# The order of seven products: A12 B21 moved from ahead of U + S3 T3 to behind it, and A12 split into high and low parts together with A22

## The chip, the cores and the metric

The kernel runs on one core of one Trainium2 chip. The metric is device time in microseconds, from the start of the program to its end, as the median of several runs. A program has five engines that work side by side, each through its own queue and in that queue's order: TensorE (matmuls and the loads of their stationary operand), VectorE, ScalarE, GpSimd and SyncE. SyncE's queue issues the loads of the weights. They wait for each other by semaphores. Matmul results go to PSUM, which has 8 banks of 128 x 512 fp32 here; everything else lies in SBUF.

## The reference

The reference is a small decoder trunk: 2 layers, 512 tokens, width 1024, hidden width 2816. A layer is half an FFN, a mixer (gated linear attention in the first layer, stick-breaking attention in the second) and half an FFN again, each on a normalised input. So there are four FFNs:

```python
def swiglu(h, w_gate, w_up, w_down):
    return (jax.nn.silu(h @ w_gate) * (h @ w_up)) @ w_down

for i in range(DEPTH):
    x = x + 0.5 * swiglu(rmsnorm(x, ffn1_norm[i]), ffn1_w_gate[i], ffn1_w_up[i], ffn1_w_down[i])
    h = rmsnorm(x, mix_norm[i])
    y = gla_mixer(h, ...) if i % 2 == 0 else sb_mixer(h, ...)
    x = x + y
    x = x + 0.5 * swiglu(rmsnorm(x, ffn2_norm[i]), ffn2_w_gate[i], ffn2_w_up[i], ffn2_w_down[i])
return rmsnorm(x, final_norm)
```

All inputs and outputs are float32.

## The kernel before, in words

**Three matmuls for one.** Activations are kept transposed, features by tokens (128 x 512 tiles). To be close to float32, every operand is split into a high and a low part in the fast matmul type (fp32r): ScalarE casts the high part (L126 for weights), VectorE subtracts it from the original to get the low part (L127). A product is then three matmuls: high x high, low x high, high x low.

**The feed.** All weight work stands in one long list of entries (`feed.q`). An entry has units (pieces of a raw weight chunk, or sums of pieces, to be split) and a body, a generator whose `yield`s divide its matmuls into steps. `Feed.start` (L139) starts the next entry: it splits the units of up to three entries ahead, as long as no more than four large units (1024 elements a partition) are in hand, makes the sums of four ahead and issues the loads of six ahead, which go to the SP queue (L91). Large split weights have four buffers for the high and four for the low parts (tags "wh", "wl"); a unit under 1024 elements goes to a single small buffer, "vh" and "vl", one of each (L116, L117). A raw chunk of 1 MB has two buffers.

**Who sets the order.** A planner orders the instructions of each engine when the program is built, by priority in program order and by its own estimate of when things are ready. For TensorE in the seven-product chunks the order is given: `feed.entries(n, True)` (L173) pins each step's TensorE instructions behind the last matmul of the step before (`issue_after`). ScalarE and VectorE are not pinned there.

**The seven-product chunks.** In an FFN, 9 of the 11 gate chunks and 9 of the 11 up chunks (256 columns each) are computed with seven products of half-size blocks instead of eight: 72 chunks in the four FFNs. `seven` (L664) cuts a chunk's weights into A11 and A12 (first 128 columns; first and second half of the input features) and A21, A22 (last 128 columns), and the tokens into two halves of 256. Each product is 4 feature tiles x 3 matmuls = 12 matmuls with 256 columns. S1 to S4 are sums of blocks of the weights (`sums_12`, `sums_34`), T1 to T4 sums of blocks of the input, made once in each FFN. Three accumulators are used, each half a bank: w, q and z. The steps, by line of the kernel before:

| product | accumulator | then |
|---|---|---|
| A11 B11 (L714) | w, new | ScalarE copies w into z (L715) |
| S1 T1 (L717) | q, new | ScalarE copies q into o1 (L718) |
| S2 T2 (L720) | w, added: U | ScalarE copies w into o0 (L721) |
| A12 B21 (L723) | z, added to the copy | the gate: SiLU on ScalarE (L701) or a multiply on VectorE (L704) |
| S3 T3 (L731) | w, added: U + S3 T3 | ScalarE copies w into u3 (L733), VectorE adds it to o1 (L734) |
| S4 B22 (L736) | q, added | VectorE adds q to o0 (L737), gates |
| A22 T4 (L743) | w, added | gate |

The first four are `body_1`, an entry with the units [A11 and A12 together, S1 and S2]; the last three are `body_2`, the next entry, with the units [S3 and S4, A22]. A22 is 512 elements a partition and goes to the small buffer. The accumulators take the 8 banks in turn (L44). Where the entry before a chunk is not of this kind, the very first matmul uses a 128 x 128 copy of its weights cast for it alone (`lead`, L129 to L133).

**What stands between the chunks.** Down projections: `down` entries (24 matmuls of 512 columns, L313), and, for one hidden group in each FFN, `seven_down` (L331), which also has seven products (L367), two entries, and an A22 of 512 elements that goes to the same small buffer and is used in its last step. It comes in two parts in each FFN; part 0 is followed at once by the next gate chunk, part 1 by a `down` entry.

Of the kernel before, what the change touches and what calls it, by code (L numbers as in the profile page):

```python
# [18 lines left out]
P = 128  # L19
T = 512  # L20
D = 1024
KD = D // P
# [6 lines left out]
NEAR, NEAR_MOVING = 16, 48  # L29
# [3 lines left out]
def decoder(ctx: ExitStack, tc: tile.TileContext, a: dict, out: bass.AP):  # L33
# [13 lines left out]
    def psum(name, tag=None):  # L47
        if tag is None:
            tag = order[turn_[0] % 8]
            turn_[0] += 1  # L50
        return pp.tile([P, T], F32, tag=tag, bufs=banks[tag], name=name)
# [130 lines left out]
    feed = Feed()  # L182
# [405 lines left out]
    class FFN:  # L588
# [75 lines left out]
        def seven(self, ch, group=None):  # L664

            H = T // 2
            s12, v = [None], {}  # L670

            def sums_12(t):
                s = s12[0] = self.tp.tile([P, KD, P], F32, tag="s", bufs=4, name="s12")
                nc.vector.tensor_tensor(out=s[:, 0:4], in0=t[:, 0:4, P:], in1=t[:, 4:8, P:], op=ALU.add)
                nc.vector.tensor_tensor(out=s[:, 4:8], in0=s[:, 0:4], in1=t[:, 0:4, 0:P], op=ALU.subtract)
                return s

            def sums_34(t):
                s = self.tp.tile([P, KD, P], F32, tag="s", bufs=4, name="s34")
                nc.vector.tensor_tensor(out=s[:, 0:4], in0=t[:, 0:4, 0:P], in1=t[:, 0:4, P:], op=ALU.subtract)  # L680
                nc.vector.tensor_tensor(out=s[:, 4:8], in0=t[:, 4:8, 0:P], in1=s12[0][:, 4:8], op=ALU.subtract)
                return s

            def prod(o, w, w0, b, first=True, lead=None):
                for j in range(4):
                    bh, bl = b(j)
                    wh, wl = w[0][:, w0 + j], w[1][:, w0 + j]
                    for n, (l_, r_) in enumerate(((wh, bh), (wl, bh), (wh, bl))):
                        if lead is not None and j + n == 0:
                            l_ = lead  # L690
                        st["pe"] = nc.tensor.matmul(  # L691
                            o, l_, r_, start=first and j + n == 0, stop=j == 3 and n == 2, skip_group_check=True
                        ).ins

            def half(k0, c):
                return lambda j: (st["h"][k0 + j][:, c * H : c * H + H], st["l"][k0 + j][:, c * H : c * H + H])

            def gate(o, c, t):

                if group is None:  # L700
                    st["silu"] = nc.scalar.activation(o[:, c : c + H], t, AF.Silu).ins  # L701
                else:
                    g = self.gates[0 if o is v["o"][0] else 1]
                    nc.vector.tensor_tensor(out=o[:, c : c + H], in0=t, in1=g[:, c : c + H], op=ALU.mult)  # L704

            def body_1(W):


                ax, s = W
                v["w"], v["q"] = psum("ps_w"), psum("ps_q")  # L710
                z = psum("ps_z")[:, 0:H]
                w, q = (v[n][:, 0:H] for n in "wq")
                o0, o1 = v["o"] = [self.tp.tile([P, T], F32, tag="t", name=n) for n in ("o0", "o1")]
                prod(w, ax, 0, half(0, 0), lead=entry.first if lead else None)  # L714
                nc.scalar.copy(z, w)  # L715
                yield
                prod(q, s, 0, lambda j: self.t_half(0, j))  # L717
                nc.scalar.copy(o1[:, H:T], q)  # L718
                yield
                prod(w, s, 4, lambda j: self.t_half(1, j), first=False)  # L720
                nc.scalar.copy(o0[:, H:T], w)  # L721
                yield
                prod(z, ax, 4, half(4, 0), first=False)  # L723
                gate(o0, 0, z)
                yield

            def body_2(W):
                s, a22 = W
                w, q = (v[n][:, 0:H] for n in "wq")
                o0, o1 = v["o"]  # L730
                prod(w, s, 0, lambda j: self.t_half(2, j), first=False)  # L731
                u3 = self.tp.tile([P, H], F32, tag="c", bufs=1, name="u3")
                nc.scalar.copy(u3, w)  # L733
                nc.vector.tensor_tensor(out=o1[:, H:T], in0=u3, in1=o1[:, H:T], op=ALU.add)  # L734
                yield
                prod(q, s, 4, half(4, 1), first=False)  # L736
                nc.vector.tensor_tensor(out=o0[:, H:T], in0=q, in1=o0[:, H:T], op=ALU.add)  # L737
                gate(o0, H, o0[:, H:T])
                if group is not None:
                    close_0(o0)  # L740
                gate(o1, H, o1[:, H:T])
                yield
                prod(w, a22, 0, lambda j: self.t_half(3, j), first=False)  # L743
                gate(o1, 0, w)
                if group is not None:
                    close_1(o0, o1)
                    del self.gates[:2]
                else:
                    self.gates += [o0, o1]
                yield  # L750

            def close_0(o0):
                if group in self.DOWN_SEVEN:
                    self.close_first(o0, group)
                else:
                    self.close(o0, group)

            def close_1(o0, o1):
                if group in self.DOWN_SEVEN:
                    self.close_second(o0, o1, group)  # L760
                else:
                    self.close(o1, group)


            lead = feed.q[-1].place != NEAR
            entry = Entry([(ch, lambda t: t[:, :, 0:P], KD, P), (ch, sums_12, KD, P)], body_1, NEAR, lead)
            feed.q.append(entry)
            feed.q.append(Entry([(ch, sums_34, KD, P), (ch, lambda t: t[:, 4:8, P:], 4, P)], body_2, NEAR))

        def t_half(self, i, j):  # L770

# [963 lines left out]
```

## Time and profile before

| | |
|---|---|
| time, median of 3 runs | 1848.96 us (1847.21 to 1850.33) |
| the profiled execution's own time | 1846.76 us |
| its span, first to last instruction | 1844.9 us |
| granted TensorE clock, mean | 0.999 |
| TensorE busy | 1829.8 us, 12188 matmuls |
| weight loads busy | 1651.2 us |
| VectorE busy | 1477.4 us |
| ScalarE busy | 1039.4 us |
| GpSimd busy | 8.7 us |

How to read it: busy time is the time in which an engine executed at least one instruction; matmuls overlap, so their starts tell the pace better than their durations. PE is TensorE's matmuls, PEld its weight loads, DVE VectorE, ACT ScalarE, POOL GpSimd, SP SyncE. A row of a group gives the line, the engine, the operation, the tiles (output <- inputs) and the count. "[0.72 <-ACT u L733]" behind an instruction says that its engine was idle for 0.72 us before it and that the ScalarE instruction of line 733, which writes u, let it go on. L126 <- raw is a cast of weights as loaded, L126 <- s one of a sum.

### The profile page before, as it was taken

To read this page: it belongs to the slowest core of one execution; us is meant where nothing else is said; L and a number is where in the kernel's file an instruction comes from. 1 tells how busy PE (TensorE), PEld (TensorE's weight loads), DVE (VectorE), ACT (ScalarE), POOL (GpSimd) and SP (SyncE) were. 2 spreads that over 40 slices of the span, in tenths; PEclk is the share of its full clock that TensorE was granted. 3 is DMA by queue.
4 is the path that set the end of the run, shared out by engine and by line. 5 is a ranking of instruction groups with operands and counts; after the bars stand their busy time and mean duration, and the time that the engine had idled before them with its cause. 6 is when DMAs were issued, how large, how long until landed. Compare 5 with 4: busy or idle time off the path is not lost.

```text
span 1844.9 us, 29917 instructions
## 1 busy us (share of the span) xinstructions
PE 1829.8 (99%) x12188; PEld 1651.2 (89%) x12188; DVE 1477.4 (80%) x2345; ACT 1039.4 (56%) x1782; POOL 8.7 (0%) x20
## 2 busy tenths in 40 slices
PE   8999999999999999999999999999999999999998
PEld 7999989889888899999889999998888788999997
DVE  8999776776787989877798997676878779897775
ACT  6556445444555556544555555455888755664454
POOL 0000000100000000000000000000000000000000
PEclk9999999999999999999999999999999999999999
DMA  5333333221223333333233233322222123333321
GB/s 162 121 119 115 103 115 113 81 69 47 69 69 114 92 110 97 126 103 104 86 109 115 92 115 115 100 85 80 69 69 61 65 92 93 114 124 103 118 80 69
DMA packets 177645, 179.16 MB, mean 97 GB/s; under 512 B 4130, under 2 KB 168020, under 8 KB 177508
## 3 DMA queue, kind: packets, MB, share of 16 engines
q1 hardware_dynamic: 176800, 176.18, 30.4%
q8 instruction: 95, 1.56, 0.4%
q0 software_dynamic: 608, 1.05, 0.2%
q14 instruction: 42, 0.34, 0.1%
q10 hardware_dynamic: 100, 0.03, 0.0%
HBM read 175.17 MB, written 2.10 MB: 96 GB/s over the span
## 4 chain that ended last, share of the span: by engine, by line
PE 89%; DVE 7%; DMA 3%; ACT 1%; issue 1%; SPq 0%; ACTq 0%; DVEq 0%
PE ps_d L66 20%; PE ps_w L691 18%; PE ps_f L66 18%; PE ps_q L691 9%; PE ps_t L66 5%; PE ps_z L691 5%; PE ps_b L66 4%; DVE wl L127 2%; DMA raw<-in_ffn_w_up_dram 2%; PE ps_w L367 1%; PE ps_S L66 1%; PE ps_z L1314 1%; PE ps_bt L66 1%; PE ps_oT L1376 1%; DMA raw<-in_ffn_w_gate_dram 1%; PE ps_T L1361 1%
## 5 line engine op out<-in xcount | busy, mean ns | idle before, releaser
L127 DVE TENSOR_TENSOR wl<-raw,wh 128x1024 fp32r<-128x1024 f32 x242 | 256.9, 1065 | 88.2 <-ACT wh L126 53.8
L126 ACT CAST wh<-raw 128x1024 fp32r<-128x1024 f32 (+1 forms) x242 | 223.2, 923 | 152.7 <-PE ps_d L66 44.4
L691 PE MATMUL ps_w<-th,wh 128*128 128x256 f32 x864 | 239.9, 278 | 2.3 <-ACT u L733 1.6
L691 PE MATMUL ps_w<-tl,wh 128*128 128x256 f32 x864 | 238.9, 276 | 0.0
L691 PE MATMUL ps_w<-th,wl 128*128 128x256 f32 x864 | 238.9, 276 | 0.0
L127 DVE TENSOR_TENSOR wl<-s,wh 128x1024 fp32r<-128x1024 f32 x160 | 195.4, 1223 | 49.3 <-PE ps_z L691 37.6
L126 ACT CAST wh<-s 128x1024 fp32r<-128x1024 f32 x160 | 168.2, 1052 | 113.2 <-PE ps_d L66 28.9
L66 PE MATMUL ps_d<-hh,wl 128*128 128x512 f32 x544 | 212.1, 390 | 0.0
L66 PE MATMUL ps_d<-hh,wh 128*128 128x512 f32 x544 | 211.9, 390 | 0.0
L66 PE MATMUL ps_d<-hl,wh 128*128 128x512 f32 x544 | 211.6, 389 | 0.0
L66 PE MATMUL ps_f<-xh,wh 128*128 128x512 f32 x432 | 172.7, 400 | 0.1
L66 PE MATMUL ps_f<-xl,wh 128*128 128x512 f32 x432 | 169.5, 392 | 0.0
L66 PE MATMUL ps_f<-xh,wl 128*128 128x512 f32 x432 | 168.9, 391 | 0.0
L691 PEld LDWEIGHTS ps_w<-th,wh 128*128 128x128 f32 x864 | 162.4, 188 | 4.1 <-ACT u L733 3.3
L691 PEld LDWEIGHTS ps_w<-tl,wh 128*128 128x128 f32 x864 | 162.2, 188 | 0.0
L691 PEld LDWEIGHTS ps_w<-th,wl 128*128 128x128 f32 x864 | 162.2, 188 | 0.0
L126 ACT CAST wh<-rawd 128x1024 fp32r<-128x1024 f32 (+1 forms) x84 | 85.1, 1014 | 121.3 <-PE ps_d L66 82.6
L322 DVE SCALAR_TENSOR_TENSOR x<-ps_d,x 128x512 f32<-128x512 f32 x152 | 102.7, 689 | 56.7 <-PE ps_d L66 56.2
L127 DVE TENSOR_TENSOR wl<-rawd,wh 128x1024 fp32r<-128x1024 f32 (+1 forms) x84 | 98.3, 1174 | 41.6 <-ACT wh L126 24.4
L66 PEld LDWEIGHTS ps_d<-hl,wh 128*128 128x128 f32 x544 | 102.1, 188 | 21.5
L66 PEld LDWEIGHTS ps_d<-hh,wh 128*128 128x128 f32 x544 | 102.1, 188 | 20.3
L66 PEld LDWEIGHTS ps_d<-hh,wl 128*128 128x128 f32 x544 | 102.1, 188 | 19.7
(348 smaller groups left out, 4880.2 us busy)
## 6 DMA issues: line engine op xcount, KB each, us to landing
raw<-in_ffn_w_gate_dram SPq DMA_DIRECT2D x43, 1024.0 KB, 5.4
raw<-in_ffn_w_up_dram SPq DMA_DIRECT2D x43, 1024.0 KB, 5.4
rawd<-in_ffn_w_down_dram SPq DMA_DIRECT2D x84, 512.0 KB, 3.6
raw<-in_gla_w_in_dram SPq DMA_DIRECT2D x12, 1024.0 KB, 5.3
raw<-in_sb_w_in_dram SPq DMA_DIRECT2D x16, 512.0 KB, 3.7
raw<-in_gla_w_out_dram SPq DMA_DIRECT2D x4, 1024.0 KB, 5.0
raw<-in_sb_w_in_dram SPq DMA_DIRECT2D x4, 1024.0 KB, 5.1
raw<-in_sb_w_out_dram SPq DMA_DIRECT2D x4, 1024.0 KB, 5.0
```

The costliest lines, as they stand in the source:

```text
L66: st["pe"] = nc.tensor.matmul(ps, l, r, start=first, stop=last).ins
L126: st["cut"] = nc.scalar.copy(h, r).ins
L127: nc.vector.tensor_tensor(out=l, in0=r, in1=h.bitcast(F32), op=ALU.subtract)
L322: nc.vector.scalar_tensor_tensor(out=xs[k], in0=ps, scalar=0.5, in1=xs[k], op0=ALU.mult, op1=ALU.add)
L367: st["pe"] = nc.tensor.matmul(ps, l_, r_, start=first and c + n == 0, stop=c == 1 and n == 2, skip_group_check=True).ins
L691: st["pe"] = nc.tensor.matmul(o, l_, r_, start=first and j + n == 0, stop=j == 3 and n == 2, skip_group_check=True).ins
L1314: nc.tensor.matmul(o_, l_, r_, start=first, stop=last, skip_group_check=True)
L1361: nc.tensor.transpose(ps[:, c0 : c0 + P], ys[yb][:, yc + j * P : yc + (j + 1) * P], ident)
L1376: nc.tensor.matmul(po[e * 64 : e * 64 + 64, j * P : T], self.v[j][:, c : c + 64], self.wt[p, e][bk][:, c0 : c0 + n], start=j == 0, stop=j ...
```

## The change

A12 B21 moves from the end of `body_1` to `body_2`, where it stands as a step of its own between U + S3 T3 and S4 B22. `body_1` has three products then and `body_2` four; z is kept between them in `v["z"]`. With it A12 changes its unit: the first entry splits A11 alone (4 x 128 = 512 elements, which goes to the small buffer) with S1 and S2; the second splits S3 and S4, and A12 with A22 as one piece of 4 x 256 = 1024 elements, a large buffer. `prod` gets a column offset `c0` so that A22 is found in the second 128 columns of that piece. The number of matmuls, casts, subtractions, sums and loads stays, and so do the total elements that are split. `seven_down` is not touched.

```diff
-            def prod(o, w, w0, b, first=True, lead=None):
+            def prod(o, w, w0, b, first=True, lead=None, c0=0):
                 for j in range(4):
                     bh, bl = b(j)
-                    wh, wl = w[0][:, w0 + j], w[1][:, w0 + j]
+                    wh, wl = (t[:, w0 + j, c0 : c0 + P] for t in w)
...
             def body_1(W):
-                ax, s = W
+                a11, s = W
                 v["w"], v["q"] = psum("ps_w"), psum("ps_q")
-                z = psum("ps_z")[:, 0:H]
+                z = v["z"] = psum("ps_z")[:, 0:H]
...
-                prod(w, ax, 0, half(0, 0), lead=entry.first if lead else None)
+                prod(w, a11, 0, half(0, 0), lead=entry.first if lead else None)
                 nc.scalar.copy(z, w)
                 yield
...
                 prod(w, s, 4, lambda j: self.t_half(1, j), first=False)
                 nc.scalar.copy(o0[:, H:T], w)
                 yield
-                prod(z, ax, 4, half(4, 0), first=False)
-                gate(o0, 0, z)
-                yield
 
             def body_2(W):
-                s, a22 = W
+                s, a2 = W
...
                 prod(w, s, 0, lambda j: self.t_half(2, j), first=False)
                 u3 = self.tp.tile([P, H], F32, tag="c", bufs=1, name="u3")
                 nc.scalar.copy(u3, w)
                 nc.vector.tensor_tensor(out=o1[:, H:T], in0=u3, in1=o1[:, H:T], op=ALU.add)
+                yield
+
+                prod(v["z"], a2, 0, half(4, 0), first=False)
+                gate(o0, 0, v["z"])
                 yield
                 prod(q, s, 4, half(4, 1), first=False)
...
-                prod(w, a22, 0, lambda j: self.t_half(3, j), first=False)
+                prod(w, a2, 0, lambda j: self.t_half(3, j), first=False, c0=P)
                 gate(o1, 0, w)
...
-            entry = Entry([(ch, lambda t: t[:, :, 0:P], KD, P), (ch, sums_12, KD, P)], body_1, NEAR, lead)
+            entry = Entry([(ch, lambda t: t[:, 0:4, 0:P], 4, P), (ch, sums_12, KD, P)], body_1, NEAR, lead)
             feed.q.append(entry)
-            feed.q.append(Entry([(ch, sums_34, KD, P), (ch, lambda t: t[:, 4:8, P:], 4, P)], body_2, NEAR))
+            feed.q.append(Entry([(ch, sums_34, KD, P), (ch, lambda t: t[:, 4:8], 4, 256)], body_2, NEAR))
```

## The prediction

> **What bounds the kernel now.** I read the page's first part, then what TensorE waits for, then the line of the seven-product chunks (L691) and the ScalarE copies that read its accumulators. First the page and the waits of TensorE (engine, line, releaser: us in total, times, longest):
>
> ```profile
> span 1844.9 us, 29917 instructions
> PE 1829.8 (99%) x12188; PEld 1651.2 (89%) x12188; DVE 1477.4 (80%) x2345; ACT 1039.4 (56%) x1782; POOL 8.7 (0%) x20
> PEclk9999999999999999999999999999999999999999
> ```
> ```profile
> PE ps_x L1571 <- DMA x<-in_x_dram: 4.3, 2, 3.8
> PE ps_w L691 <- ACT u L733: 1.6, 3, 0.7
> PE ps_f L1596 <- ACT wh L1541: 0.6, 1, 0.6
> PE ps_w L691 <- ACT ps_z L715: 0.4, 2, 0.2
> ```
>
> TensorE is busy for 99% of the span and hardly waits once the inputs have landed. So a change pays only by fewer or denser matmuls, and every microsecond for which TensorE is made to wait is added whole. This change keeps all matmuls. What it moves are the copies which stand between two uses of one accumulator. The same line with the waits of weight loads added (times in ns min/median/max; then idle us, times):
>
> ```profile
> L691 PE MATMUL ps_w<-th,wh x864: 276/276/388, 71.6 to 1806.6; 128*128 128x256 f32 x173
>   ACT u L733: 4.9, 10
>   ACT ps_z L715: 1.2, 4
> ```
>
> Now one chunk's second half of step 1, where U (the third product) ends and A12 B21 (into z) begins, with the ScalarE copy that reads U out of w:
>
> ```profile
> 122.30 0.28 PE L691 MATMUL ps_w<-tl,wh 128*128 128x256 f32 x1
> 122.41 0.28 PE L691 MATMUL ps_z<-nh,wh 128*128 128x256 f32 x1
> ...
> 122.61 0.37 ACT L721 COPY o<-ps_w 128x256 f32<-128x256 f32 x1 [0.99 <-PE ps_w L691]
> ...
> 123.66 0.28 PE L691 MATMUL ps_z<-nl,wh 128*128 128x256 f32 x1
> 123.77 0.28 PE L691 MATMUL ps_w<-th,wh 128*128 128x256 f32 x1
> ```
>
> Matmuls start 0.113 us apart (122.30, 122.41), and a product of 12 takes 1.36 (122.41 to 123.77). The copy of U runs from 122.61 to 122.98, while TensorE fills z; w is next wanted at 123.77, 0.79 after the copy's end. That product is the whole cover of the copy.
>
> **The change part by part.**
>
> *A12 B21 leaves the place between U and U + S3 T3.* The products then run w (A11), q (T1), w (U), w (U + S3 T3), z, q, w. S3 T3 accumulates onto the w that the copy in L721 is still to read, so its first matmul has to wait for that copy, with nothing between. Each step's TensorE instructions are pinned behind the last matmul of the step before, so the planner has nothing to put there. How TensorE starts again after such a wait is seen at the longest one of today, at the u3 copy (L733):
>
> ```profile
> 734.34 0.28 PE L691 MATMUL ps_q<-nl,wh 128*128 128x256 f32 x1
> 734.71 0.30 ACT L132 CAST w<-raw 128x128 fp32r<-128x128 f32 x1 [1.72 <-DMA raw<-in_ffn_w_up_dram]
> 734.92 0.37 ACT L733 COPY u<-ps_w 128x256 f32<-128x256 f32 x1
> 735.34 0.38 PE L691 MATMUL ps_w<-th,wh 128*128 128x256 f32 x1 [0.72 <-ACT u L733]
> 735.56 0.28 PE L691 MATMUL ps_w<-th,wl 128*128 128x256 f32 x1
> 735.67 0.28 PE L691 MATMUL ps_w<-tl,wh 128*128 128x256 f32 x1
> ```
> ```profile
> 735.33 0.19 PEld L691 LDWEIGHTS ps_w<-th,wh 128*128 128x128 f32 x1 [0.91 <-ACT u L733]
> ```
>
> The copy ends at 735.29 and the matmul starts at 735.34: 0.05. The second one follows after 0.22 instead of 0.113: 0.11 more. Put together, from the start of U's last matmul: copy begins after 0.31 (122.30 to 122.61), takes 0.37, restart 0.05: 0.73, less the 0.113 that pass anyhow, is 0.62; with the slow first matmul 0.73 us a chunk. The number of chunks is the number of these copies:
>
> ```profile
> L721 ACT COPY o<-ps_w x72: 366/374/378, 73.2 to 1801.8; 128x256 f32<-128x256 f32 x72
>   PE ps_w L691: 68.5, 68
> ```
> ```profile
> L733 ACT COPY u<-ps_w x72: 364/374/378, 75.9 to 1804.5; 128x256 f32<-128x256 f32 x72
>   PE ps_w L691: 12.6, 32
> ```
>
> 72 x 0.73 = **52.6 us**. In 68 of 72 ScalarE stood waiting for the product when it ended, so the copy started at once. For the 4 late ones I count half a 1.05 us cast each (the 1024-wide cast, row below): 2 us. The other bound is the behaviour of the u3 copy, which is late in 40 of 72: 40 x 0.5 = 20. I take **2**, because L721 itself is the nearest row.
>
> Behind the waiting matmul the whole TensorE queue stands still; nobody else works for the end of the kernel meanwhile, so nothing is won back, and VectorE and ScalarE only gain slack.
>
> On the 0.11 of the restart there is a rule that speaks for less. The Trainium skill, "TensorE: Matmul & The Clock Gate", section "Step-by-step: what each phase is for", says that the queue pulls a weight load ahead of matmuls in flight; by that the weights would be there when the copy ends, the sum would be 72 x 0.11 = 7.9 us smaller, and the row above, where the weight load itself starts only at 735.33, speaks against it.
>
> *A12 B21 enters between U + S3 T3 and S4 B22.* The u3 copy now has 24 matmuls as cover instead of 12. At 735.34 the wait was 0.72 of idle; with 1.36 more cover it is gone, and so are its like: 10 waits, 4.9 us of idle that overlaps in part between loads and matmuls. I take **-4**; bounds 0 and -4.9 (plus 10 restarts of 0.11). z is written 1.36 later, and its reader (gate, L704 or L701) too; nobody on TensorE waits for it before eight further accumulators have been handed out, so 0. If z's bank came round early, the cost would be one such copy wait, at most another 0.7 where it happens.
>
> *A11 is split by itself, A12 together with A22.* The elements stay 512 + 1024 + 1024 + 1024 a chunk; no cast, subtraction or DMA is added or dropped. What moves is the single small buffer ("vh"/"vl", one of each): before it held A22, wanted by a chunk's last product, now A11, wanted by its first. The seven-product down projection still keeps its own A22 there and uses it in its last product. Where a chunk follows such a pair at once (part 0, once in each of 4 FFNs), A11 cannot be cast until that product has ended, and TensorE waits for cast and subtraction. The first of the four places today (TensorE, ScalarE, VectorE):
>
> ```profile
> 146.78 0.28 PE L367 MATMUL ps_w<-t,wh 128*128 128x256 f32 x1
> 146.89 0.28 PE L691 MATMUL ps_w<-nh,wh 128*128 128x256 f32 x1
> 147.00 0.28 PE L691 MATMUL ps_w<-nh,wl 128*128 128x256 f32 x1
> ```
> ```profile
> 145.73 1.05 ACT L126 CAST wh<-raw 128x1024 fp32r<-128x1024 f32 x1 [0.99 <-PE ps_q L367]
> 147.09 0.62 ACT L126 CAST wh<-raw 128x512 fp32r<-128x512 f32 x1 [0.31 <-PE ps_w L367]
> ```
> ```profile
> 147.51 0.76 DVE L373 SCALAR_TENSOR_TENSOR x<-ps_w,x 128x256 f32<-128x256 f32 x2
> 148.17 0.70 DVE L127 TENSOR_TENSOR wl<-raw,wh 128x512 fp32r<-128x512 f32 x1
> ```
>
> Today this small cast and subtraction are hidden, as the chunk wants them six products later. After the change the second matmul wants wl: ready at 148.87, start at 148.92 in place of 147.00, 1.9 us, and 0.1 for the restart: 2.0. If VectorE took the subtraction right after the cast (147.71 + 0.70 = 148.41), 1.6. Four places: 6.4 to 8; if the planner found a way round, 0. I take **8**, as VectorE's adds (L373) stand in its queue as shown.
>
> Elsewhere the small buffer comes free after a chunk's first product and is wanted by the next chunk's first: six products of cover, 8.2 us, against 0.62 + 0.70. When that cast runs straight after the first product it stands ahead of the z copy (L715), which has 1.36 of cover and needs 0.31 + 0.36 + 0.05, 0.72; 0.62 more still fits. Cost 0; a 1.05 cast in front as well would break it, and for that I keep 5 us in the range.
>
> *Queues.* The last reader of the raw chunk is now a 1024-wide subtraction in place of the 512-wide one, about 0.5 us longer, and the SP queue waits for just such readers before it loads the next chunk:
>
> ```profile
> SPq L91 <- DVE wl L127: 1581.3, 183, 28.5
> ACT w L132 <- DMA raw<-in_ffn_w_up_dram: 9.7, 8, 1.7
> ```
>
> The lead cast L132 waits for a landing in 8 places and blocks ScalarE there, as at 734.71. Every chunk also takes 0.73 us longer, which gives the load more than the 0.5 that it loses: 0; bounds -4 and +4 (8 x 0.5). The POOL queue issues nothing here.
>
> **Sum.** 52.6 + 2 - 4 + 8 = 58.6. The profiled execution took 1846.76 us (span 1844.9 and 1.9 around it): 1905.4. That is 2.2 below the median of the runs shown (1848.96), so at the level of the median I predict **1907 us**, 3.1% slower.
>
> **The rivals.**
>
> *The copy comes late as a rule.* ScalarE does its queue in order; if the planner, which now sees TensorE stop, puts one of the 1.05 us casts ahead of L721 in half the chunks, half of it is added: 72 x 0.5 x 0.5 = 18 more, 1925. For it: the u3 copy is late in 40 of 72. Against it: L721 in only 4.
>
> *Only the copy stall counts.* The planner finds no wait at the down pairs (8 less) and the weights of the next matmul are in place when the copy ends, so that the slow restart falls away (72 x 0.11 = 7.9 less): 1907 - 15.9 = 1891. Against it stand the single buffer and the row at 735.33.
>
> *Not slower: the gap is filled.* If the planner set matmuls of z's product ahead of S3 T3, the copy would be covered again; from 6 of the 12 on (0.62 / 0.113) nothing would be left of the 54.6, and the time would be 1848.96 - 4 + 8 = 1853, within 0.2% or little over, and 1845 if the small buffer costs nothing as well. For it: the planner does order the instructions. Against it: the pins by step, and today's order w, q, w, z, w, q, w, which the starts above follow.
>
> *The clock falls.* A pause of 0.62 in every chunk could let the granted clock sink. The chunks hold 72 x 84 matmuls x 0.113 = 683 us; a tenth of it at half rate would add 68: 1975. Against it: after 0.72 of idle at 735.34 the matmuls go on 0.11 apart, and the granted clock is at 9 tenths or more in every slice. The Trainium skill, "TensorE: Matmul & The Clock Gate", section "A second HAM failure mode: psum-queue depth-cycling", tells of a kernel that such short pauses between groups of matmuls made swing between half and full rate; no run here shows it so far.
>
> **How the numbers follow.** Forecast 0.72 (its own range 1897 to 1915); late copies 0.13; only the copy stall 0.08; gap filled 0.04; clock 0.03. Leaving out the last two and the outer part of the late copies gives 1889 to 1926: the lower end takes the copy stall alone, the upper the late ones. A measurement of this kernel can tell about 0.2% (3.7 us) from no change; of the gap-filled case I count 0.02 as within it, 0.01 as faster, 0.01 as slower: faster 0.01, same 0.02, slower 0.97.
>
> **What would show it.** TensorE's waits get a new first row: ps_w of L691 released by the copy in L721, 72 times (or nearly), some 0.6 us each, TensorE's busy share falls by two to three points, and the first matmul of S3 T3 starts 0.05 after that copy. The u3 waits (L733) are gone. At four places a first matmul of L691 after L367 waits for the cast of L126 and then for L127. The page's matmul durations stay at 276. Wrong I would be if another product stood between U and S3 T3, if ScalarE reached L721 late in many chunks, or if the small buffer's wait were longer because VectorE comes to it late.

## The result

The changed kernel takes 1917.26 us (median of 5 runs, 1916.58 to 1918.43), the kernel before 1847.28 (5 runs). The ratio is 1.0373, with a 95% interval of 1.0361 to 1.0385: 70 us, or 3.7%, slower. The prediction was 1907 us, 3.1%, with a range of 1889 to 1926.

The page of the changed kernel: the same matmuls, a longer span.

```profile
span 1914.3 us, 29909 instructions
PE 1852.8 (97%) x12188; PEld 1656.9 (87%) x12188; DVE 1491.7 (78%) x2345; ACT 1035.9 (54%) x1782; POOL 8.8 (0%) x20
PEclk9999999999999999999999999999999999999999
```

What TensorE waits for after the change (us in total, times, longest us):

```profile
PE ps_w L691 <- ACT o L721: 33.5, 72, 0.5
PE ps_w L691 <- ACT ps_z L715: 8.1, 11, 1.4
PE ps_x L1572 <- DMA x<-in_x_dram: 4.1, 2, 3.7
PE ps_w L691 <- DVE wl L127: 3.5, 4, 1.0
PE ps_w L691 <- ACT wh L126: 2.8, 4, 0.7
```

The first row is new: 72 times, once a chunk, released by the copy of U. The fourth and fifth rows are new too, 4 times each. The second was 0.4 us in 2 waits. The u3 copy has left the list. These are only the times in which no matmul ran at all; matmuls overlap, so the starts tell the whole price. The place in a chunk, matmuls first, then weight loads, then ScalarE:

```profile
125.76 0.28 PE L691 MATMUL ps_w<-tl,wh 128*128 128x256 f32 x1
126.50 0.38 PE L691 MATMUL ps_w<-th,wh 128*128 128x256 f32 x1 [0.46 <-ACT o L721]
126.72 0.29 PE L691 MATMUL ps_w<-th,wl 128*128 128x256 f32 x1
```
```profile
126.50 0.19 PEld L691 LDWEIGHTS ps_w<-th,wh 128*128 128x128 f32 x1 [0.66 <-ACT o L721]
```
```profile
126.07 0.37 ACT L721 COPY o<-ps_w 128x256 f32<-128x256 f32 x1 [1.43 <-PE ps_w L691]
```

U's last matmul starts at 125.76, the copy runs from 126.07 to 126.44, S3 T3 starts at 126.50 and its second matmul 0.22 later. Matmuls that wait for nothing start 0.113 apart; measured by that, the first one is 0.63 late and the second another 0.11.

The starts of all 504 products, each against 0.113 us a matmul (0.227 where the one before has 512 columns), give the balance in us. "Into" is the first matmul's delay, "inside" that of the other eleven, both summed over the 72 chunks. The table has the four products that changed; each of the other three is within 0.4 us of before:

| | before, into + inside | after, into + inside | difference |
|---|---|---|---|
| A11 B11 (first product) | 0.01 + 0.13 | 3.48 + 5.10 | +8.4 |
| S2 T2 (third, waits for the z copy) | 0.77 + 0.62 | 11.32 + 2.23 | +12.2 |
| S3 T3 (waits for the U copy after the change) | 0.03 + 0.27 | 45.19 + 9.29 | +54.2 |
| A22 T4 (last, waits for the u3 copy) | 3.03 + 1.08 | 0.00 - 0.02 | -4.1 |

Together +70.7; the spans differ by 69.4 (1914.3 - 1844.9).

### The profile page after: what moved, and what is told of

It reads as the page before. It is cut to its first block, busy times and chain, and to the rows that moved or that the text cites. A ratio compares the mean times of both kernels' runs of the same rounds, so it can differ in the third digit from the quotient of the medians.

```text
span 1914.3 us, 29909 instructions
## 1 busy us (share of the span) xinstructions
PE 1852.8 (97%) x12188; PEld 1656.9 (87%) x12188; DVE 1491.7 (78%) x2345; ACT 1035.9 (54%) x1782; POOL 8.8 (0%) x20
## 4 chain that ended last, share of the span: by engine, by line
PE 84%; DVE 8%; DMA 3%; ACT 3%; issue 1%; SPq 0%; DVEq 0%; ACTq 0%
PE ps_d L66 19%; PE ps_f L66 17%; PE ps_w L691 17%; PE ps_q L691 8%; PE ps_t L66 5%; PE ps_z L691 4%; PE ps_b L66 4%; DVE wl L127 3%; DMA raw<-in_ffn_w_up_dram 2%; PE ps_S L66 1%; PE ps_z L1315 1%; DMA raw<-in_ffn_w_gate_dram 1%; ACT o L721 1%; PE ps_bt L66 1%; PE ps_w L367 1%
## 5 line engine op out<-in xcount | busy, mean ns | idle before, releaser
L126 ACT CAST wh<-raw 128x512 fp32r<-128x512 f32 (+1 forms) x242 | 223.3, 923 | 167.4 <-PE ps_f L66 37.3
L127 DVE TENSOR_TENSOR wl<-raw,wh 128x512 fp32r<-128x512 f32 (+1 forms) x242 | 256.1, 1060 | 66.5 <-ACT wh L126 65.6
L691 PE MATMUL ps_w<-th,wh 128*128 128x256 f32 x864 | 248.2, 287 | 42.1 <-ACT o L721 33.5
L126 ACT CAST wh<-s 128x1024 fp32r<-128x1024 f32 x160 | 168.1, 1050 | 162.3 <-PE ps_q L691 62.4
L127 DVE TENSOR_TENSOR wl<-s,wh 128x1024 fp32r<-128x1024 f32 x160 | 195.3, 1221 | 61.2 <-ACT wh L126 59.1
L126 ACT CAST wh<-rawd 128x1024 fp32r<-128x1024 f32 x84 | 84.8, 1010 | 116.1 <-PE ps_d L66 68.9
L127 DVE TENSOR_TENSOR wl<-rawd,wh 128x1024 fp32r<-128x1024 f32 x84 | 97.6, 1170 | 24.6 <-ACT wh L126 21.8
```

What stands on the lines that cost most here:

```text
L126: st["cut"] = nc.scalar.copy(h, r).ins
L127: nc.vector.tensor_tensor(out=l, in0=r, in1=h.bitcast(F32), op=ALU.subtract)
L691: st["pe"] = nc.tensor.matmul(o, l_, r_, start=first and j + n == 0, stop=j == 3 and n == 2, skip_group_check=True).ins
```

## The experiments

Medians in us; "before" is the kernel before, measured beside each run on the same chip. There it took between 1845.25 and 1848.58, so a difference from the changed kernel's 1917.26, which was measured beside 1847.28, is good to about 2 us; the spans and the starts of one trace are sharper.

**One half alone: the order.** A12 B21 moves from the end of body_1 into body_2, behind U + S3 T3; the split stays as it was:

```diff
 order_only, against before
-                z = psum("ps_z")[:, 0:H]
+                z = v["z"] = psum("ps_z")[:, 0:H]
+                v["ax"] = ax
...
-                prod(z, ax, 4, half(4, 0), first=False)
-                gate(o0, 0, z)
-                yield
...
+                yield
+                prod(v["z"], v["ax"], 4, half(4, 0), first=False)
+                gate(o0, 0, v["z"])
```

> A12 B21 stands between U + S3 T3 and S4 B22 as after the change, but A11 and A12 are split together and A22 by itself, as before it. Copy theory (each U copy is uncovered, and the u3 waits go): 72 waits on L721 of about 0.74 us with the restart, 54 us, less 4: about 1898 us. It expects no stall at the four places behind the seven-product down projection, and hardly any wait for the z copy (L715), if those late z copies come from the A11 cast. Rival (the z copies are late because the new order moves ScalarE's and VectorE's other work): the waits for L715 stay at about 12 us, and the time is about 1909.

1900.75 against 1845.25, ratio 1.0300 (1.0284 to 1.0315). The waits of TensorE:

```profile
PE ps_w L691 <- ACT o L722: 34.1, 72, 0.6
PE ps_x L1572 <- DMA x<-in_x_dram: 4.2, 2, 3.7
PE ps_w L691 <- ACT ps_z L716: 3.1, 7, 1.1
```

(L722 and L716 are the U copy and the z copy here; one line was added.) The order alone costs 55 us, and by the starts of the products 54 of it lie at S3 T3. The four places behind the down pairs cost nothing. The z copies were not quite as expected: 5.4 us by the starts, 1.4 before. In 5 of the 8 latest cases ScalarE casts the closing tiles of the hidden units ahead of the z copy, in 2 it loads a table, as it did before the change.

**The other half alone: the split.** The products run as in the kernel before:

```diff
 split_only, against after
             def body_2(W):
                 s, a2 = W
...
+                prod(v["z"], a2, 0, half(4, 0), first=False)
+                gate(o0, 0, v["z"])
+                yield
                 prod(w, s, 0, lambda j: self.t_half(2, j), first=False)
...
-                prod(v["z"], a2, 0, half(4, 0), first=False)
-                gate(o0, 0, v["z"])
-                yield
                 prod(q, s, 4, half(4, 1), first=False)
```

> The split of the changed kernel (A11 alone, A12 with A22), but A12 B21 is the first step of the second entry, so that the products run in the order of the kernel before: w, q, w, z, w, q, w. Copy theory: no wait on L721 at all; the four places behind the down pairs cost 8.6 us; if the A11 cast is what makes the z copies late, they cost another 6 to 12, and the u3 waits of about 4 us stay: 1856 to 1868. Rival (the split is what costs the 70 us, by feeding TensorE late): 1900 or more.

1867.17 against 1845.25, ratio 1.0121 (1.0104 to 1.0138): at the upper end of what was expected. The waits:

```profile
PE ps_w L691 <- ACT ps_z L715: 8.8, 13, 1.2
PE ps_x L1571 <- DMA x<-in_x_dram: 4.6, 2, 3.8
PE ps_w L691 <- DVE wl L127: 3.6, 4, 1.1
PE ps_w L691 <- ACT wh L126: 2.8, 4, 0.7
```

No wait on the U copy, so that wait belongs to the order. By the starts, the first products lose 8.8 and the third ones 15.3. One thing was not expected: the u3 waits are gone here as well, without the added cover. I come back to it below.

**The copy wait taken away, all else left.** S3 T3 and A22 T4 use an accumulator of their own, so that U is missing from their sums:

```diff
 fresh_w, against after
+                w = psum("ps_w")[:, 0:H]
-                prod(w, s, 0, lambda j: self.t_half(2, j), first=False)
+                prod(w, s, 0, lambda j: self.t_half(2, j))
```

> The changed kernel, but S3 T3 and A22 T4 go to a fresh accumulator of their own, so no matmul waits for the U copy. U is left out of the sums in o1 by that, so this kernel computes something else. All copies, casts and matmuls stay. Copy theory: the 72 waits on L721 vanish, 54.5 us less than the changed kernel: about 1863 us, with the four places and the z copy waits still there. Rival (TensorE would wait at S3 T3 anyway, for the split weights): a wait of about the same size appears there with another releaser, and the time stays above 1890.

1869.77 against 1845.25, ratio 1.0132 (1.0117 to 1.0147). Expected was 1863. The wait on L721 is gone and nothing has taken its place at S3 T3 (1.0 us by the starts). The missing 7 us lie mostly at the four places behind the down pairs, where the wait for L127 grew by 2.3:

```profile
PE ps_w L691 <- ACT ps_z L715: 7.2, 10, 1.6
PE ps_w L691 <- DVE wl L127: 5.8, 4, 1.5
PE ps_x L1573 <- DMA x<-in_x_dram: 4.2, 2, 3.7
PE ps_w L691 <- ACT wh L126: 2.8, 4, 0.7
```

Behind the longer stop the granted clock fell at three of the four places. The first of them (four matmuls, then the stretch from 152 to 155 us, whose last three figures are the granted clock, the busy share of the DMA engines and GB/s):

```profile
149.74 0.38 PE L691 MATMUL ps_w<-nh,wh 128*128 128x256 f32 x1 [0.71 <-ACT wh L126]
151.54 0.58 PE L691 MATMUL ps_w<-nh,wl 128*128 128x256 f32 x1 [1.41 <-DVE wl L127]
151.91 0.42 PE L691 MATMUL ps_w<-nl,wh 128*128 128x256 f32 x1
152.13 0.42 PE L691 MATMUL ps_w<-nh,wh 128*128 128x256 f32 x1
```
```profile
152.00:155.00 3.00, 3.00 (x18) 3.00 (x18) 0.74 (x3) 0.71 (x2) 0.00 (x0) 0.58 0.74 245
```

For some 15 matmuls the starts are then 0.21 apart in place of 0.113, at a clock of 0.58 here, 0.55 from 1070 to 1073 and 0.56 from 1656 to 1659. By the starts this costs 4.6 us in the three places together. The mean granted clock of this kernel's four runs is 0.996 to 0.997, that of the kernel before 0.999.

**The small buffer left to A11.** The down projection's A22 takes a large one:

```diff
 down_large, against after
-                    few = n * m < 1024
+                    few = n == 4 and n * m < 1024
...
-                used += sum(n * m >= 1024 for _, _, n, m in e.units)
+                used += sum(n == 2 or n * m >= 1024 for _, _, n, m in e.units)
```

> The changed kernel, but A22 of the seven-product down projection goes to a large buffer, so that the small one serves A11 alone. Small-buffer theory: the stalls at the four places behind part 0 of the down projection vanish, 8.6 us less than the changed kernel: about 1908.7 us. Rival (the stall there is VectorE's backlog of adds, not the buffer): the first product still waits for its low part, at least 1 us at each place, and the time stays at 1913 or above.

1904.97 against 1845.25, ratio 1.0323 (1.0308 to 1.0339): 12 us below the changed kernel by the medians, 11.4 by the spans of the two traces. In the list of TensorE's waits the rows of L126 and L127 are gone, and the first products lose nothing. Some 3 us more than expected came from the z copies (10.7 by the starts, 13.6 in the changed kernel).

**The copy doubled.** The same U copy twice, before and after the change:

```diff
 twice_before, against before; twice_after, against after
                 nc.scalar.copy(o0[:, H:T], w)
+                nc.scalar.copy(o0[:, H:T], w)
```

> The kernel before, with the U copy of L721 issued twice, one behind the other (72 more copies of 0.37 us on ScalarE; the same result). Copy theory: U's copy is covered there by A12 B21 with 0.79 us to spare, and a second copy takes about 0.3, so nothing is added: within 4 us of the kernel before. Rival (ScalarE's work itself counts, covered or not): 72 x 0.3 = 22 us more.

> The changed kernel, with the same second U copy. Copy theory: TensorE waits for both, and each chunk takes the step from one ScalarE copy to the next longer, 0.27 to 0.31 us: 72 times that is 19 to 22 us, about 1937 us. Rival (TensorE waits at S3 T3 for something else that ends at about the same time): no change, 1917.

Both sizes were missed: before the change 1894.7 against 1848.58 (ratio 1.0251, 1.0237 to 1.0265), after it 1997.53 (ratio 1.0814, 1.0797 to 1.0830), 80 us above the changed kernel. The second copy did not follow the first: the planner set a large cast between the two, in all 72 chunks of the doubled kernel before and in 65 of the doubled kernel after. The first kernel shows it so (ScalarE, then TensorE):

```profile
125.03 0.37 ACT L721 COPY o<-ps_w 128x256 f32<-128x256 f32 x1 [0.99 <-PE ps_w L691]
125.30 1.05 ACT L126 CAST wh<-s 128x1024 fp32r<-128x1024 f32 x1
126.25 0.37 ACT L722 COPY o<-ps_w 128x256 f32<-128x256 f32 x1
```
```profile
126.08 0.28 PE L691 MATMUL ps_z<-nl,wh 128*128 128x256 f32 x1
...
126.67 0.39 PE L691 MATMUL ps_w<-th,wh 128*128 128x256 f32 x1 [0.32 <-ACT o L722]
```

So this pair doesn't measure a second copy, but it shows that the wait is for the last reader of U, and how little it takes to lose the cover: the second copy ends at 126.62, 1.22 later than the first, and the cover of 0.79 is used up.

**The A11 cast behind the z copy.** Where two chunks follow each other directly, the second one's first entry (A11, S1 and S2) is split one entry later:

```diff
 a11_behind, against after
             for e in self.q[i : i + 3]:
+                if e is not self.q[i] and all(x.units[0][2] * x.units[0][3] < 1024 for x in (e, self.q[i])):
+                    break
                 used += sum(n * m >= 1024 for _, _, n, m in e.units)
```

> The changed kernel, but where two chunks follow each other directly, the next chunk's first entry (A11, S1 and S2) is split one entry later, so its A11 cast stands behind the z copy in the program's order and no longer ahead of it. If the A11 cast with another cast behind it is what makes the z copies late where no closing cast is in front, the waits for L715 fall from about 13.6 us to about 8, and the time to about 1911. Rival (the late z copies come from whatever the planner finds ready, and splitting later makes the next chunk's S1 and S2 late): the waits stay or new ones appear at the first and second product, 1917 or more.

1908.66, ratio 1.0323 (1.0309 to 1.0337): 8.6 below the changed kernel. The third products lose 6.4 in place of 13.6, and the first ones 7.4 in place of 8.6. In the changed kernel the worst of these places looks like this (ScalarE, then TensorE): a large cast and the A11 cast stand ahead of the z copy, and the third product starts 1.6 late.

```profile
1106.10 1.04 ACT L126 CAST wh<-s 128x1024 fp32r<-128x1024 f32 x1
1107.03 0.62 ACT L126 CAST wh<-raw 128x512 fp32r<-128x512 f32 x1
1107.55 0.37 ACT L715 COPY ps_z<-ps_w 128x256 f32<-128x256 f32 x1
```
```profile
1106.25 0.28 PE L691 MATMUL ps_q<-tl,wh 128*128 128x256 f32 x1
1107.98 0.39 PE L691 MATMUL ps_w<-th,wh 128*128 128x256 f32 x1 [1.45 <-ACT ps_z L715]
```

**The lead cast off ScalarE.** In the kernel before:

```diff
 lead_pool, against before
-                        nc.scalar.copy(first, r[:, 0, 0:P])
+                        nc.gpsimd.tensor_copy(first, r[:, 0, 0:P])
```

> The kernel before, with the order and the split as they were; only the lead cast of 128 x 128 weights (L132), which in 8 places stands in ScalarE's queue waiting for a load while the u3 copy waits behind it, is done on GpSimd. Theory (that cast causes the u3 waits): the 4 us of u3 waits go, about 1842 us against 1846. Rival: the GpSimd cast is slower and holds up the first matmul of the 40 chunks that use it, slower by up to 40 x 0.5 = 20 us.

1846.18 against 1848.58, ratio 0.9987 (0.9978 to 0.9995). The u3 copy holds up no matmul any more, so the u3 waits of the kernel before came from the lead cast that waited for its load. Of the 4 us that were expected 2.4 came; by the starts the third products lose 3.1 here, 1.4 before. The kernel is 0.13% faster than the kernel before.

**The copy made shorter.** 16 of 256 columns:

```diff
 small_copy, against after
-                nc.scalar.copy(o0[:, H:T], w)
+                nc.gpsimd.memset(o0[:, H + 16 : T], 0.0)
+                nc.scalar.copy(o0[:, H : H + 16], w[:, 0:16])
```

> The changed kernel, but ScalarE copies only 16 of U's 256 columns into o0; the other 240 are set to zero by GpSimd, so the result lacks them. Nothing else changes. ScalarE's rows give 0.37 us for 256 columns, 0.62 for 512 and 1.05 for 1024, some 0.9 ns a column, so the copy falls to about 0.16. Copy theory: each of the 72 waits shrinks by that 0.21, 15 us: about 1902. Rival (the wait is set by the way there and back, not by the copy's length, or by another releaser): 1917.

1903.66 against 1847.90, ratio 1.0303 (1.0285 to 1.0320): 13.6 below the changed kernel. The copy, and below it who waited for it (us in total, times):

```profile
L722 ACT COPY o<-ps_w x72: 172/173/173, 73.3 to 1857.7; 128x16 f32<-128x16 f32 x72
  PEld ps_w L691: 33.0, 72
  PE ps_w L691: 18.8, 72
```

The copy fell by 0.20 (0.372 to 0.173), TensorE's wait from 33.5 to 18.8, and by the starts from 0.63 to 0.43 a chunk. The wait follows the copy one for one.

**Both repairs, with the changed order and with the old one.** The edits of down_large and a11_behind together; then the same with A12 B21 as the first step of the second entry, as in split_only; then with the lead cast on GpSimd too.

> The changed order and split, with both small repairs: the down projection's A22 in a large buffer, and A11 of a directly following chunk split one entry later. Theory: what is left is the U copy's 54.5 us less the 4 of the u3 waits, and some 6 us at the z copies behind closing casts: about 1900, no better than the order alone moved (1900.75). Rival (the two repairs rob each other of a large buffer): first products wait for split weights, 1908 or more.

> The products in the order of the kernel before (w, q, w, z, w, q, w), with the changed split and both small repairs. Theory (the split costs only through the small buffer and the casts ahead of the z copies, and by itself removes the u3 waits, as its run alone had none): no waits on the U copy, none at first products, about 4 us at the z copies, no u3 waits: within 4 us of the kernel before. Rival (the split itself feeds TensorE later): 1855 or more.

> The same with the lead cast of 128 x 128 weights on GpSimd as well. Theory: the u3 waits are gone already, so the lead cast no longer matters: equal to the run without it within 2 us. Rival (the lead cast also holds up z copies): about 2 to 4 us faster, some 1844.

With the changed order: 1898.47 against 1847.90, ratio 1.0273 (1.0257 to 1.0288). The waits:

```profile
PE ps_w L693 <- ACT o L723: 33.5, 72, 0.5
PE ps_x L1574 <- DMA x<-in_x_dram: 4.5, 2, 3.9
PE ps_f L1598 <- ACT wh L1543: 0.6, 1, 0.6
```

With the old order: 1844.88 against 1845.74, ratio 0.9995 (0.9986 to 1.0004), no difference that can be told; with the lead cast on GpSimd 1844.01, ratio 0.9991 (0.9983 to 1.0000). The waits with the old order and the lead cast on ScalarE (U copy and small buffer are absent):

```profile
PE ps_x L1573 <- DMA x<-in_x_dram: 3.8, 1, 3.8
PE ps_f L1598 <- ACT wh L1543: 0.8, 1, 0.8
PE ps_w L693 <- ACT ps_z L717: 0.7, 2, 0.4
```

So with the repairs the changed split costs nothing that can be told, and the changed order keeps the wait for the U copy. The two kernels differ in the order alone, 1898.47 against 1844.88; by the starts 53.6 of that lie at S3 T3 and 1.4 at the z copies.

Why the u3 waits go with the split alone is suggested by the SP queue: the load of the same chunk in the kernel before, and in the one with the mended split and the old order:

```profile
81.04 0.37 SPq L91 DMA_DIRECT2D raw<-in_ffn_w_up_dram  x1
```
```profile
79.86 0.37 SPq L91 DMA_DIRECT2D raw<-in_ffn_w_up_dram  x1
```

With the changed split it is issued 1.2 us earlier. Before, the last reader of the raw chunk was A22's small cast and subtraction, which waited for the one small buffer until the chunk before had ended; now it is A12 with A22, which goes to a large buffer. ScalarE's lead cast waits about as long for the loads as before (10.0 us in 8 places, 9.7 before), but it ends earlier in the chunk. In the 8 places the loads land 6.4 to 7.3 us after the chunk's first matmul, 7.3 to 8.6 before, and the u3 copies are at most 0.34 late, 0.47 to 1.62 before; their cover of one product, 1.36 for a need of 0.73, takes that. That the buffer is what held the subtraction up is read from the code and from this one place; no run tests it by itself.

## Why the prediction came out as it did

The direction and the main mechanism held, and the time lies in the stated range of 1889 to 1926. It lies 2 us above the 1897 to 1915 that the forecast was given for itself. The room above that was kept for late U copies, which did not come; late z copies took it, for which 5 us had been kept and which cost 12. That the range held was in that part luck. By its own steps:

- *A12 B21 leaves the place between U and U + S3 T3: 52.6 + 2.* Right. S3 T3 loses 54.5 by the starts, 54.2 more than before: a chunk, 0.63 at the first matmul (0.62 was worked out) and 0.13 behind it (0.11 was worked out, and that much comes at the second matmul). Taking the order alone, the accumulator apart and the shorter copy show it from three sides. No U copy came late: ScalarE waited for the product in all 72. So the 2 us kept for late copies were not spent, and it is luck that the 0.01 and 0.02 a chunk by which the other two parts were short come to nearly the same. The rival with copies late as a rule did not come true here; the doubled copy shows what a large cast ahead of U's last reader costs.
- *The slow restart of 0.11.* Right. The saving that was worked out from the Trainium skill ("TensorE: Matmul & The Clock Gate", "Step-by-step: what each phase is for") did not come: the weight load of the waiting matmul starts only with it, at 126.50, after 0.66 of idle. The rows of those who waited for the U copy say why. The loads wait for it themselves, in all 72 places:

```profile
L721 ACT COPY o<-ps_w x72: 372/372/373, 72.8 to 1870.4; 128x256 f32<-128x256 f32 x72
  PEld ps_w L691: 47.6, 72
  PE ps_w L691: 33.5, 72
```

So these runs do not contradict the rule; they show that a load which waits for the same copy does not run ahead.
- *The clock falls (a rival).* Not in the changed kernel: the granted clock stayed at 9 tenths or more in every slice in spite of 72 more pauses of some 0.46 us. It is no empty rival, though. In the kernel with the accumulator apart the clock fell at three places, to 0.55 to 0.58 for some microseconds.
- *A12 B21 enters ahead of S4 B22: -4.* The size was right, 4.1. The reason was not the whole of it: the order alone removes the waits, as was said, but the split alone removes them too, in which the next chunk's load starts sooner. Both halves of the change remove them, and they can be saved only once.
- *The small buffer: 8.* Right, 8.4; it came at four places, as named. VectorE took one large subtraction first, as was feared (152.22, with A11's at 153.35):

```profile
152.72 0.39 PE L691 MATMUL ps_w<-nh,wh 128*128 128x256 f32 x1 [0.71 <-ACT wh L126]
154.09 0.38 PE L691 MATMUL ps_w<-nh,wl 128*128 128x256 f32 x1 [0.99 <-DVE wl L127]
```
```profile
152.22 1.22 DVE L127 TENSOR_TENSOR wl<-s,wh 128x1024 fp32r<-128x1024 f32 x1
153.35 0.68 DVE L127 TENSOR_TENSOR wl<-raw,wh 128x512 fp32r<-128x512 f32 x1
```

- *The A11 cast ahead of the z copy: 0, with 5 kept in the range.* This is the term that was mis-sized: 12.2. The step saw that the A11 cast stands ahead of the z copy and that it fits alone. The z copy was over 0.3 late in 40 of 72 chunks, 8 before; in 20 of the 40 the A11 cast stood there alone, and the third product lost at most 0.01. But the step counted one cast and not what else the planner sets there: in 10 of the others a large cast stood ahead of the copy, in 8 the closing casts, in 2 a table load. Moving the A11 cast took 7.2 of the 12.2 away. What is left, about 5, also shows with the order alone (4.0); the closing casts in front of the copy are seen there, and why they come later was not tried.
- *Queues: 0.* The sign of the reasoning was wrong. I said that the raw chunk would be released 0.5 later because its last subtraction is longer; with the changed split and the old order the load shown above is issued 1.2 earlier.

The sum was short by 70.0 - 58.6 = 11.4 us, and the z copies are 12.2.

## What to carry to other kernels

An accumulator that is read out in the middle of its accumulation needs work on another accumulator behind each such read: count the reads and the products that can cover them (here three gaps in w and three products outside w), and moving a product for one gap uncovers another at the full price of way there, copy, way back and restart. When a unit moves to a single buffer, look at who else uses that buffer and when, and look at everything that may stand ahead of a copy in an in-order queue, not only at the one cast that you move. A repair that makes a load start earlier can do the same as more cover. And look at the granted clock of a run before its time is read as waits alone: in one of the runs here a quarter of a percent was lost to it.

## What the runs showed of the hardware beside that

A ScalarE copy of 128 x 16 fp32 took 0.173 us and one of 128 x 256 0.372: 0.2 for 240 columns. If the time grows evenly between the two, about 0.16 of each such copy doesn't depend on its length; that is an estimate from these two rows.

TensorE's granted clock fell for some microseconds in two of the runs. With the accumulator apart it fell behind idle times of 0.71 and 1.41 to 1.53 us with one matmul between them, at three of the four places; the fourth, with 0.71 and 1.44, kept its clock. In the doubled kernel after the change it fell to 0.52 (132 to 135 us) behind 0.57 and 1.83, and to 0.57 (1142 to 1146 us) behind 0.71 and 0.79. In the changed kernel the same 0.71 and 0.79, at 1093.37, left it at 1.00. So these runs give no length of a stop from which the clock falls. They do show that a stop of some 0.46 in every chunk did not lower it.
